# Scores of a pair of heads: block diagonal keys against two matmuls of 64 rows on two row groups

## The chip, the cores and the metric

The kernel runs on one core of one Trainium2 chip. The metric is the device time of one execution in microseconds (us). The kernel before was run three times: 2077.02, 2077.57 and 2078.26 us, median 2077.57 us. A profile of one execution shows which instruction ran on which engine and when. The engines are PE (TensorE, matmuls) with PEld (its weight loads, which overlap the matmuls), DVE (VectorE), ACT (ScalarE), POOL (GpSimd) and SP (SyncE, which issues transfers).

## The reference, cut to what matters

The network has four layers on 256 tokens of width 1024. Each layer is a feed-forward part, a token mixer and a second feed-forward part. Layers 0 and 3 use the mixer called DSA, layer 1 uses FoX, layer 2 uses MLA. All have 16 heads; DSA and FoX have 64 numbers per head, MLA has 96 in its queries and keys. What the change touches are scores of queries against keys:

```python
def causal_block_attention(q, k, v, scale, cum=None):            # FoX, MLA
    ...
        s = jnp.einsum('bqhd,bkhd->bhqk', q[:, lo:hi], k[:, :hi]).astype(jnp.float32) * scale
        ...
        p = jax.nn.softmax(jnp.where(mask, s, -jnp.inf), axis=-1).astype(v.dtype)
        outs.append(jnp.einsum('bhqk,bkhd->bqhd', p, v[:, :hi]))

def dsa_mixer(x, w_in, w_out, cos_p, sin_p):                      # DSA
    ...
        dots = jnp.einsum('bqhd,bkd->bqhk', qib, ki).astype(jnp.float32) * (IDX_DIM ** -0.5)
        idx_score = jnp.einsum('bqh,bqhk->bqk', wib, jax.nn.relu(dots))   # 8 index heads, one key
        ...
        _, sel = lax.top_k(idx_score, topk)
        ...
        logits = jnp.einsum('bqhd,bqkhd->bhqk', qb, ks).astype(jnp.float32) * scale
```

DSA has two kinds of scores: those of the indexer (8 index heads of 64, all against one shared key), whose weighted sum picks the 64 best keys of each query, and those of the 16 heads themselves.

## The kernel before, in words

Every product is a float32 product made of three passes: an operand is split into a high part and a low part (`split`, L189: ACT copies the high part, then DVE subtracts to get the low part), and the passes high·high, high·low, low·high are summed in PSUM (`mm3`, L157 to L161). Weights come from memory through SP's queue into `raw` tiles and are split too (`unit`, L127 to L147: ACT L144, DVE or POOL L145). Tokens are two tiles of 128 (t = 0, 1).

Heads are treated in eight pairs, two pairs to a group. `heads` (L439) runs the pairs one after the other. For pair p+1 it emits the score matmuls, then pieces of the projections of later groups and of the output product (the tables `PLAN_D`, `PLAN_F`, `OUTS` say how many), then for pair p the transposes of the softmax weights (`turn`), the softmax of pair p+1, more pieces, and the product with the values (`weigh`). What is emitted is then put in an order for each engine by a scheduler; every engine works through its own list in that order and waits where an operand is not ready.

One matmul of 128 rows holds both heads of a pair: rows 0 to 63 of the array are the first head's 64 numbers, rows 64 to 127 the second's. The queries of the pair are the stationary operand (128 rows, 128 queries). The keys are the moving operand and are block diagonal: `new_kz` (L494) gives a tile in which a head's rows are zero in the other head's columns (two POOL memsets, L497 and L498), and `put_kz` (L501) writes the keys of each head into its own block with a split of its own. So a pair takes, for each token tile, three matmuls with 2·128 columns (t = 0) or 2·256 columns (t = 1), into one bank of PSUM per token tile (`pair_scores`, L506). The scores of DSA's indexer use the same function, four pairs of index heads for each t; ACT then applies a ReLU to both heads at once (L560) and DVE adds them up with their weights (L564, L566). PSUM has two sets of four banks here, named psa and psb; scores, transposes and value products share psb.

Of the kernel before, what the change touches and what calls it, by code (L numbers as in the profile page):

```python
# [16 lines left out]
F32 = mybir.dt.float32  # L17
# [5 lines left out]
P = 128  # L23
D = 1024
SEQ = 256
# [6 lines left out]
HD = 64  # L32
# [19 lines left out]
class Net:  # L52
# [39 lines left out]
    def consts(self):  # L92
        """What the first products need; the rest comes in late_consts."""
# [7 lines left out]
        # the activation table and the tensor engine's clock are brought up while the loads run  # L101
# [67 lines left out]
    def flush(self):  # L169
        """Emits the transposes of x that wait for a place among other products."""  # L170
# [4 lines left out]
    def proj(self, us, t, out, flush=None):  # L175
        """out[tokens of tile t, n] = x @ w over the K tiles of us."""
# [6 lines left out]
    def projb(self, us, i, out, k0=0):  # L183
        """out[columns i*128.. of w, tokens] = (x @ w) transposed; us are the K tiles from k0."""
# [36 lines left out]
    def layer_norm(self, t, acc, mult, eps, last=False):  # L221
        """x <- LN(mult * x + acc); scaling the argument by two and eps by four changes nothing."""
# [677 lines left out]
```

## Time and profile before

| what | value |
|---|---|
| median of three runs | 2077.57 us |
| the profiled execution, first to last instruction | 2077.2 us |
| PE busy | 2021.1 us (97%), 13430 matmuls |
| PEld busy | 1853.2 us (89%) |
| DVE busy | 1271.0 us (61%) |
| ACT busy | 1030.3 us (50%) |
| POOL busy | 320.7 us (15%) |
| weights and other transfers | 362.98 MB, mean 175 GB/s |

The page gives the span of the profiled execution alone and no time around it; the runs' median is 0.4 us above that span. A busy time is the union of an engine's instructions; matmuls overlap each other, so the time that PE needs for one of them is read from start to start and not from its duration. The share of the whole span hides stages: the first DSA mixer's part from the indexer to its last pair is from about 226 to 345 us of the span, FoX's pairs start at about 772 us, the second DSA mixer's indexer at about 1757 us.

### The profile page before, as it was taken

Reading aid. Unit: us, or ns where it says so; the run is one execution under the profiler, and the core shown is the slowest. Engines: PE = TensorE matmul, PEld = TensorE weight load, DVE = VectorE, ACT = ScalarE, POOL = GpSimd, SP = SyncE. Lnnn points to the kernel's source line nnn. Section 1 sums busy time; section 2 is a strip of 40 time slices with the busy share of each in tenths; the row PEclk is TensorE's granted clock in tenths of the full one; section 3 lists DMA queues with packets and bytes.
Section 4 is the critical chain, followed back from the end, with each engine's and each line's share of the span. In section 5 each row is a group of like instructions: output and inputs, shape, how many; then the busy total and the mean of one; then the engine's idle time right before and its main releaser. Section 6 shows DMA issues by size and latency. Waiting matters only on the chain.

```text
span 2077.2 us, 34193 instructions
## 1 busy us (share of the span) xinstructions
PE 2021.1 (97%) x13430; PEld 1853.2 (89%) x13430; DVE 1271.0 (61%) x2069; ACT 1030.3 (50%) x1714; POOL 320.7 (15%) x454
## 2 busy tenths in 40 slices
PE   9999998999999998999999999899999999989998
PEld 8999986999899987799989998689989999978997
DVE  6455889544644469855465456964465546887453
ACT  5443476444444357644444436754444444675441
POOL 0002542000100145200110014400020005430000
PEclk9999999999999999999999999999999999999999
DMA  9754534665656454565665543566656564347550
GB/s 304 226 184 138 153 122 155 214 188 176 212 183 188 150 162 155 185 208 184 183 203 182 186 121 105 180 214 185 187 178 208 187 180 131 119 125 237 189 184 21
DMA packets 253025, 362.98 MB, mean 175 GB/s; under 512 B 11856, under 2 KB 204128, under 8 KB 252864
## 3 DMA queue, kind: packets, MB, share of 16 engines
q1 hardware_dynamic: 252080, 358.30, 54.7%
q0 software_dynamic: 784, 2.51, 0.4%
q8 instruction: 105, 1.72, 0.3%
q14 instruction: 56, 0.46, 0.1%
HBM read 359.69 MB, written 1.06 MB: 174 GB/s over the span
## 4 chain that ended last, share of the span: by engine, by line
PE 82%; DVE 12%; ACT 3%; issue 2%; POOL 0%; DMA 0%; SPq 0%; DVEq 0%; ACTq 0%; POOLq 0%
PE psa L166 14%; PE psa L167 14%; PE psa L165 14%; PE psb L159 8%; PE psb L160 8%; PE psb L161 8%; PE psa L159 5%; PE psa L161 5%; PE psa L160 5%; DVE slot L145 3%; DVE slot L191 2%; DVE s L406 2%; ACT s L403 1%; PE psb L202 1%; ACT slot L144 1%
## 5 line engine op out<-in xcount | busy, mean ns | idle before, releaser
L145 DVE TENSOR_TENSOR slot<-raw,slot 128x1024 fp32r<-128x1024 f32 (+4 forms) x724 | 773.1, 1089 | 617.5 <-ACT slot L144 614.9
L144 ACT CAST slot<-raw 128x1024 fp32r<-128x1024 f32 (+5 forms) x854 | 693.8, 849 | 652.0 <-issue 354.9
L166 PE MATMUL psa<-xh,slot 128*128 128x256 f32 x2496 | 707.6, 284 | 3.8 <-DVE slot L145 3.8
L165 PE MATMUL psa<-xh,slot 128*128 128x256 f32 x2496 | 707.4, 284 | 0.0
L167 PE MATMUL psa<-xl,slot 128*128 128x256 f32 x2496 | 707.1, 283 | 0.0
L166 PEld LDWEIGHTS psa<-xh,slot 128*128 128x128 f32 x2496 | 479.7, 192 | 7.6 <-DVE slot L145 4.6
L165 PEld LDWEIGHTS psa<-xh,slot 128*128 128x128 f32 x2496 | 479.6, 192 | 3.0
L167 PEld LDWEIGHTS psa<-xl,slot 128*128 128x128 f32 x2496 | 479.6, 192 | 0.0
L159 PE MATMUL psb<-slot,slot 128*128 128x512 f32 (+2 forms) x800 | 308.1, 385 | 9.0 <-DVE slot L191 4.8
L160 PE MATMUL psb<-slot,slot 128*128 128x512 f32 (+2 forms) x800 | 306.9, 384 | 1.9 <-DVE slot L191 1.9
L161 PE MATMUL psb<-slot,slot 128*128 128x512 f32 (+2 forms) x800 | 305.3, 382 | 1.2 <-DVE slot L191 1.2
L159 PE MATMUL psa<-slot,xh 128*128 128x256 f32 (+5 forms) x736 | 241.1, 328 | 0.0
L160 PE MATMUL psa<-slot,xh 128*128 128x256 f32 (+5 forms) x736 | 238.6, 324 | 0.0
L161 PE MATMUL psa<-slot,xl 128*128 128x256 f32 (+5 forms) x736 | 238.1, 324 | 0.0
L145 POOL TENSOR_TENSOR slot<-raw,slot 128x512 fp32r<-128x512 f32 (+4 forms) x130 | 183.5, 1428 | 306.1 <-ACT slot L144 297.1
L159 PEld LDWEIGHTS psb<-slot,slot 128*128 128x128 f32 (+1 forms) x800 | 150.9, 189 | 37.7 <-ACT slot L190 5.3
L78 POOL MEMSET slot<- 128x1 f32 (+1 forms) x88 | 8.5, 101 | 1118.4 <-PE psb L161 972.1
L161 PEld LDWEIGHTS psb<-slot,slot 128*128 128x128 f32 (+1 forms) x800 | 150.9, 189 | 30.9 <-DVE slot L191 1.5
L160 PEld LDWEIGHTS psb<-slot,slot 128*128 128x128 f32 (+1 forms) x800 | 151.2, 189 | 28.3 <-DVE slot L191 2.7
L159 PEld LDWEIGHTS psa<-slot,xh 128*128 128x128 f32 x736 | 140.6, 191 | 10.3 <-ACT xh L190 0.3
L160 PEld LDWEIGHTS psa<-slot,xh 128*128 128x128 f32 x736 | 140.6, 191 | 10.2
L161 PEld LDWEIGHTS psa<-slot,xl 128*128 128x128 f32 x736 | 140.4, 191 | 10.4
(150 smaller groups left out, 1696.7 us busy)
## 6 DMA issues: line engine op xcount, KB each, us to landing
raw<-in_ffn_w SPq DMA_DIRECT2D x528, 512.0 KB, 4.2
raw<-in_dsa_w_in SPq DMA_DIRECT2D x48, 512.0 KB, 3.8
raw<-in_w_out SPq DMA_DIRECT2D x32, 512.0 KB, 3.6
raw<-in_fox_w_in SPq DMA_DIRECT2D x24, 512.0 KB, 3.8
ln_g<-in_ln_g SPq DMA_DIRECT2D x12, 512.0 KB, 5.5
ln_b<-in_ln_b SPq DMA_DIRECT2D x12, 512.0 KB, 5.8
slot<-scratch_cum POOLq DMA_DIRECT2D x4, 512.0 KB, 5.4
raw<-in_mla_w_ukv SPq DMA_DIRECT2D x4, 512.0 KB, 3.9
```

The costliest lines, as they stand in the source:

```text
L144: nc.scalar.copy(h[:, c], raw[:, c])
L145: e.tensor_sub(l[:, c], raw[:, c], h[:, c].bitcast(F32))
L159: mm(out, sh, mh, start=start, stop=False)
L160: mm(out, sh, ml, start=False, stop=False)
L161: mm(out, sl, mh, start=False, stop=stop)
L165: mm(out, sh, mh, start=start, stop=False)
L166: mm(out, sl, mh, start=False, stop=False)
L167: mm(out, sh, ml, start=False, stop=stop)
L191: self.nc.vector.tensor_sub(lo, src, hi.bitcast(F32))
L202: self.nc.tensor.transpose(ps[:, i * P:(i + 1) * P], self.x[t][:, k * P:(k + 1) * P], self.ident)
L403: nc.scalar.activation(sv, sv, AF.Exp, bias=nb[:, c:c + 1], scale=scale, accum_out=l[:, c:c + 1])
L406: nc.vector.tensor_scalar(sv, sv, l[:, c:c + 1], None, op0=ALU.mult)
```

## The change

`pair_scores` no longer uses block diagonal keys. The keys of a pair lie as they come, 128 rows with both heads one above the other, and each pass is two matmuls of 64 rows: rows 0 to 63 (first head) and rows 64 to 127 (second head) of the array, each with its own weight load, and each writing its own bank of PSUM. The two token tiles of a head stand side by side in that bank (128 and 256 columns). In the indexer a call takes two banks where it took one, and the ReLU becomes two instructions, one for each bank. `new_kz` and `put_kz` go away: in DSA the queries and keys of a group are split together, in FoX the keys of a group are split at once. MLA's scores only change their form of call.

```diff
     def softmax(self, scores, bias, scale, cq=None):
-        pss = [scores(t) for t in range(NT)]
+        pss = scores(range(NT))
...
-                    nc.vector.tensor_tensor_reduce(out=sv, in0=pss[t][:, j, :], in1=bias(t, j), scale=1.0,
+                    nc.vector.tensor_tensor_reduce(out=sv, in0=pss[t][j], in1=bias(t, j), scale=1.0,
...
-    def new_kz(self, n=2):
-        """Block diagonal K of pairs: a head's rows are zero in the other head's columns."""
-        z = self.slot(2 * n, 2, SEQ, touch=False)
-        self.nc.gpsimd.memset(z[0:64, :, 1, :].bitcast(F32), 0.0)
-        self.nc.gpsimd.memset(z[64:128, :, 0, :].bitcast(F32), 0.0)
-        return z[:, :n], z[:, n:]
-
-    def put_kz(self, kz, c, src):
-        for j in range(2):
-            q = slice(64 * j, 64 * j + 64)
-            self.split(kz[0][q, :, j, c], kz[1][q, :, j, c], src[q])
-
     def pair_scores(self, qh, ql, kh, kl):
-        def scores(i):
-            ps = self.ps("b")
-            n = (i + 1) * P
-            o = ps[:, :2 * n].rearrange("p (j k) -> p j k", j=2)
-            q = slice(i * P, (i + 1) * P)
-            self.mm3(o, qh[:, q], ql[:, q], kh[:, :, :n], kl[:, :, :n], True, True)
-            return o
+        def scores(ts):
+            banks = [self.ps("b") for _ in range(2)]
+            out, o = [], 0
+            for t in ts:
+                n = (t + 1) * P
+                q = slice(t * P, n)
+                out.append([z[:, o:o + n] for z in banks])
+                o += n
+                for a, (st, mv) in enumerate(((qh, kh), (qh, kl), (ql, kh))):
+                    for j in range(2):
+                        r = slice(64 * j, 64 * j + 64)
+                        self.nc.tensor.matmul(out[-1][j], st[r, q], mv[r, :n], start=a == 0, stop=a == 2)
+            return out
         return scores
...
              self.split(qi[0][:, :, c], qi[1][:, :, c], p0.rearrange("p (k c) -> p k c", k=4))
-            self.put_kz(ki, c, p1[:, None, :P])
+            self.split(ki[0][:, c], ki[1][:, c], p1[:, :P])
...
         def index(t):
             n, sc = (t + 1) * P, scs[t]
             for i in range(4):
-                ps = self.pair_scores(qi[0][:, i], qi[1][:, i], *[z[:, 0] for z in ki])(t)
+                ps, = self.pair_scores(qi[0][:, i], qi[1][:, i], *ki)([t])
...
-                nc.scalar.activation(r[:, :, :n], ps, AF.Relu, scale=HD ** -0.5)
                 for j in range(2):
+                    nc.scalar.activation(r[:, j, :n], ps[j], AF.Relu, scale=HD ** -0.5)
...
 -                self.split(q[:, 0, :, c], q[:, 1, :, c], pt[:, 2:])
-                self.put_kz(kz, c, pt[:, :2])
+                self.split(qk[:, 0, :, c], qk[:, 1, :, c], pt.rearrange("p (k c) -> p k c", k=4))
...
 -                if isq:
-                    self.split(q[:, 0], q[:, 1], ps)
-                else:
-                    self.put_kz(kz, slice(None), ps)
+                self.split(qk[:, isq, 0], qk[:, isq, 1], ps)
```

The first place is PE's list in the first DSA mixer, where the scores of the third pair follow the value product of the first (L165 to L167). Names beginning with psb are PSUM banks. Before, the scores' last passes stand there, 256 columns for t = 0 and 512 for t = 1:

```order
L166 MATMUL psb_2960<-pth_2879,slot_2075 128x2x128
L167 MATMUL psb_2960<-ptl_2880,slot_2075 128x2x128
L160 MATMUL psb_2971<-slot_2486,slot_2489 128x256
L161 MATMUL psb_2971<-slot_2486,slot_2489 128x256
L159 MATMUL psb_2975<-slot_2486,slot_2489 128x512
L160 MATMUL psb_2975<-slot_2486,slot_2489 128x512
L161 MATMUL psb_2975<-slot_2486,slot_2489 128x512
L159 MATMUL psa_2993<-slot_2980,xh_1840 128x256
```

After the change the same place has twelve matmuls, which go to the banks of the two heads in turn:

```order
L167 MATMUL psb_2988<-ptl_2908,slot_2073 128x2x128
L508 MATMUL psb_2999<-slot_2512 128x128
L508 MATMUL psb_3000<-slot_2512 128x128
L508 MATMUL psb_2999<-slot_2512 128x128
L508 MATMUL psb_3000<-slot_2512 128x128
L508 MATMUL psb_2999<-slot_2512 128x128
L508 MATMUL psb_3000<-slot_2512 128x128
L508 MATMUL psb_2999<-slot_2512 128x256
L508 MATMUL psb_3000<-slot_2512 128x256
```

Six matmuls of 128 rows (the first of them stood a little earlier) have become twelve of 64 rows in one unbroken block. In the whole program there are 384 matmuls of 64 rows in 26 such blocks, two of them the indexers' (48 each), so that the lists change over to matmuls of 64 rows 26 times and back 26 times.

The second place is PE's list in the first indexer, where the second half of its calls begins. Before, matmuls of a projection (psa) stand between the calls:

```order
L161 MATMUL psb_2322<-slot_1968,slot_1966 128x256
L159 MATMUL psa_2382<-slot_2369,xh_1840 128x256
L159 MATMUL psb_2331<-slot_1968,slot_1966 128x512
L160 MATMUL psa_2382<-slot_2369,xh_1840 128x256
L161 MATMUL psa_2382<-slot_2369,xl_1841 128x256
L159 MATMUL psa_2382<-slot_2369,xh_1840 128x256
L160 MATMUL psb_2331<-slot_1968,slot_1966 128x512
L161 MATMUL psb_2331<-slot_1968,slot_1966 128x512
```

After the change nothing stands between them, and each call writes two banks:

```order
L508 MATMUL psb_2331<-slot_1968,slot_1966 128x128
L508 MATMUL psb_2332<-slot_1968,slot_1966 128x128
L508 MATMUL psb_2345<-slot_1968,slot_1966 128x256
L508 MATMUL psb_2346<-slot_1968,slot_1966 128x256
L508 MATMUL psb_2345<-slot_1968,slot_1966 128x256
L508 MATMUL psb_2346<-slot_1968,slot_1966 128x256
```

Seven projection matmuls that stood inside the first indexer now stand behind it.

The third place is ACT's list right behind the first indexer, where a group's queries and keys (psb_2409) are split. Before, the queries are split once and the keys twice, for the two halves of the rows:

```order
L190 CAST slot_2075<-psa_2382 128x256
L190 CAST slot_2075<-psb_2409 128x2x128
L144 CAST slot_2613<-raw_2612 128x512
L144 CAST slot_2696<-raw_2695 128x512 x2
L190 CAST slot_2072<-psb_2409 64x2x128
L190 CAST slot_2075<-psa_2420 128x256
L144 CAST slot_2703<-raw_2702 128x512
L190 CAST slot_2072<-psb_2409 64x2x128
```

After the change one instruction does it:

```order
L190 CAST slot_2073<-psa_2416 128x256
L190 CAST slot_2071<-psb_2443 128x4x128
L144 CAST slot_2713<-raw_2712 128x512 x2
L190 CAST slot_2073<-psa_2450 128x256
```

Three casts of a group's token tile are one, and the same holds for DVE's subtractions behind them.

## Rows read from the trace of the kernel before

**Rows 1.** The page: PE's busy time; columns are busy us, share, instructions.
```profile
PE 2021.1 (97%) x13430; PEld 1853.2 (89%) x13430; DVE 1271.0 (61%) x2069; ACT 1030.3 (50%) x1714; POOL 320.7 (15%) x454
```

**Rows 2.** Stretches, length; busy us (count) of PE, PEld, DVE, ACT, POOL; clock; DMA.
```profile
226.00:310.00 84.00, 78.80 (x601) 75.44 (x600) 74.52 (x218) 54.70 (x141) 38.10 (x52) 0.98 0.41 127
310.00:345.00 35.00, 29.72 (x154) 23.42 (x153) 31.96 (x77) 22.34 (x64) 7.79 (x7) 1.00 0.49 158
772.00:830.00 58.00, 50.31 (x367) 46.15 (x365) 53.06 (x140) 39.56 (x106) 34.24 (x35) 0.97 0.45 146
```

**Rows 3.** Chain of waits from 226 to 310 us, by line.
```profile
by line: DVE slot L145 18.8%; DVE slot L191 13.0%; DVE slot L566 8.6%; DVE slot L576 7.8%; issue 6.2%; DVE m L575 5.9%; PE psa L159 5.6%; PE psa L161 5.3%; PE psa L160 5.2%; DVE s L393 3.2%; ACT slot L144 2.5%; DVE ptl L191 2.4%; DVE nb L39
```

**Rows 4.** Waits of PE from 200 to 325 us: total, times, longest.
```profile
PE psb L159 <- DVE slot L191: 2.0, 1, 2.0
```

**Rows 5.** Timeline, score matmuls of the first indexer: start us, duration us, engine, line.
```profile
231.46 0.39 PE L161 MATMUL psb<-slot,slot 128*128 128x512 f32 x1
...
231.69 0.39 PE L159 MATMUL psb<-slot,slot 128*128 128x512 f32 x1
```

**Rows 6.** Timeline, weight loads that follow an idle PE, of two kinds.
```profile
229.94 0.19 PEld L159 LDWEIGHTS psb<-slot,slot 128*128 128x128 f32 x1 [1.32 <-ACT slot L190]
...
230.05 0.19 PEld L160 LDWEIGHTS psa<-slot,xh 128*128 128x128 f32 x1
...
290.46 0.14 PEld L416 LDWEIGHTS psb<-c_ident,s 128*128 128x128 f32 x1 [1.29 <-issue]
...
290.52 0.14 PEld L417 LDWEIGHTS psb<-c_ident,s 128*128 128x128 f32 x1
```

**Rows 7.** Timeline around two transposes of 16 rows in FoX (L673).
```profile
772.14 0.28 PE L167 MATMUL psa<-xl,slot 128*128 128x256 f32 x1
...
772.35 0.20 PEld L673 LDWEIGHTS psb<-c_ident,slot 16*128 16x128 f32 x2
772.35 0.29 PE L673 MATMUL psb<-c_ident,slot 16*128 16x16 f32 x2
772.57 0.19 PEld L159 LDWEIGHTS psb<-slot,slot 128*128 128x128 f32 x1
772.57 0.39 PE L159 MATMUL psb<-slot,slot 128*128 128x256 f32 x1
...
772.79 0.28 PE L160 MATMUL psb<-slot,slot 128*128 128x256 f32 x1
...
772.91 0.28 PE L161 MATMUL psb<-slot,slot 128*128 128x256 f32 x1
```

**Rows 8.** Weight loads by line and shape: count, busy us, mean ns.
```profile
L673 PEld LDWEIGHTS psb<-c_ident,slot 16*128 16x128 f32 x2 | 0.2, 136 | 0.1
...
L416 PEld LDWEIGHTS psb<-c_ident,s 128*128 128x128 f32 x16 | 2.2, 140 | 1.6 <-issue 1.5
```

**Rows 9.** DVE's subtractions of L191 by shape, 212 to 345 us, then 755 to 860.
```profile
L191 DVE TENSOR_TENSOR slot<-psb,slot 64x256 fp32r<-64x256 f32 x32 | 13.2, 418 | 1.8 <-ACT slot L190 1.3
...
L191 DVE TENSOR_TENSOR slot<-psb,slot 128x256 fp32r<-128x256 f32 x8 | 3.3, 417 | 0.2
...
L191 DVE TENSOR_TENSOR slot<-psb,slot 128x512 fp32r<-128x512 f32 x2 | 1.4, 684 | 0.0
...
L191 DVE TENSOR_TENSOR slot<-psa,slot 64x512 fp32r<-64x512 f32 x8 | 5.5, 687 | 2.5 <-ACT slot L190 2.4
...
L191 DVE TENSOR_TENSOR slot<-psa,slot 128x512 fp32r<-128x512 f32 x4 | 2.7, 685 | 3.2 <-ACT slot L190 3.1
```

**Rows 10.** Timeline of the first indexer: third and sixth ReLU, last score matmul.
```profile
230.85 0.38 ACT L560 ACTIVATE tok<-psb 128x256 f32<-128x256 f32 x1 [0.96 <-DVE slot L566]
...
233.53 0.39 PE L161 MATMUL psb<-slot,slot 128*128 128x512 f32 x1
...
233.78 0.60 ACT L560 ACTIVATE tok<-psb 128x512 f32<-128x512 f32 x1 [0.24 <-DVE slot L566]
```

**Rows 11.** POOL's memsets of key tiles in the whole span, first of two lines.
```profile
L497 POOL MEMSET slot<- 64x1024 f32 x12 | 11.4, 947 | 10.3 <-PE psa L161 9.1 <-ACT slot L144 0.8 <-PE psa L167 0.4
```

More of the change, by code (lines that the diff above doesn't have):

```diff
@@ L523, in dsa @@
         qi = qi[:, 0], qi[:, 1]
-        ki = self.new_kz(1)
+        ki = self.slot(2, SEQ)
+        ki = ki[:, 0], ki[:, 1]
         misc = self.slot(2048, dt=F32)
@@ L585, in project @@
             qw = self.cols(w_in, 256 * g, 256)
-            kz = self.new_kz()
-            qv = self.slot(2, 2, 2, SEQ)
-            q, v = qv[:, 0], qv[:, 1]
+            qk = self.slot(2, 4, SEQ)
+            v = self.slot(2, 2, SEQ)
             toks = []
@@ L598, in project @@
                 yield 1
-            ready[g] = (q, kz, v)
+            ready[g] = (qk, v)
             vals = self.values(w_in, 2 * D + 256 * g, v)
@@ L606, in project @@
                     nc.tensor.transpose(pt[:, i * P:(i + 1) * P], toks[t][:, i * P:(i + 1) * P], self.ident)
-                pt = pt.rearrange("p (k c) -> p k c", k=4)
-                self.split(q[:, 0, :, c], q[:, 1, :, c], pt[:, 2:])
-                self.put_kz(kz, c, pt[:, :2])
+                self.split(qk[:, 0, :, c], qk[:, 1, :, c], pt.rearrange("p (k c) -> p k c", k=4))
                 yield 1
@@ L613, in weights @@
             g, i = p // 2, p % 2
-            q, kz, v = ready[g]
-            rest = self.softmax(self.pair_scores(q[:, 0, i], q[:, 1, i], kz[0][:, i], kz[1][:, i]),
+            qk, v = ready[g]
+            rest = self.softmax(self.pair_scores(*(qk[:, z, y + i] for y in (2, 0) for z in range(2))),
                                  lambda t, j: sel[t], HD ** -0.5)
@@ L679, in project @@
             if g % 2 == 0:
-                both["ck"], both["q"] = self.slot(2, 4, SEQ, dt=F32), self.slot(2, 2, 2, SEQ)
-            ck, q = both["ck"][:, g % 2], both["q"][:, g % 2]
+                both["ck"] = self.slot(2, 4, SEQ, dt=F32)
+            ck, qk = both["ck"][:, g % 2], self.slot(2, 2, 2, SEQ)
             nc.gpsimd.dma_start(ck, self.a["s_cum"][4 * g:4 * g + 4].partition_broadcast(P))
-            kz = self.new_kz()
-            ready[g] = (q, kz, ck)
+            ready[g] = (qk, ck)
             for isq, o in ((0, D), (1, 0)):
@@ L691, in project @@
                         yield 1
-                if isq:
-                    self.split(q[:, 0], q[:, 1], ps)
-                else:
-                    self.put_kz(kz, slice(None), ps)
+                self.split(qk[:, isq, 0], qk[:, isq, 1], ps)
                 yield 1
@@ L699, in weights @@
             g, i = p // 2, p % 2
-            q, kz, ck = ready[g]
+            qk, ck = ready[g]
             b0 = b0s[p % 2]
@@ L708, in weights @@
             nc.vector.tensor_copy(cq, cumq[:, 2 * p:2 * p + 2, :].rearrange("p h t -> p t h"))
-            rest = self.softmax(self.pair_scores(q[:, 0, i], q[:, 1, i], kz[0][:, i], kz[1][:, i]),
+            rest = self.softmax(self.pair_scores(*(qk[:, y, z, i] for y in (1, 0) for z in range(2))),
                                  lambda t, j: b0[:, j, :] if t == 0 else cp[:, j, :], scale,
@@ L803, in weights, with scores @@
             q, k = qk[i]
-            def scores(t):
-                ps = self.ps("b").rearrange("p (j k) -> p j k", j=2)
-                c = slice(t * P, (t + 1) * P)
-                for j in range(2):
-                    self.mm3(ps[:, j], q[:, 0, j, c], q[:, 1, j, c], k[:, 0, j], k[:, 1, j], True, True)
-                return ps[:, :, :(t + 1) * P]
+            def scores(ts):
+                out = []
+                for t in ts:
+                    ps = self.ps("b").rearrange("p (j k) -> p j k", j=2)
+                    c = slice(t * P, (t + 1) * P)
+                    for j in range(2):
+                        self.mm3(ps[:, j], q[:, 0, j, c], q[:, 1, j, c], k[:, 0, j], k[:, 1, j], True, True)
+                    out.append([ps[:, j, :(t + 1) * P] for j in range(2)])
+                return out
             rest = self.softmax(scores, lambda t, j: self.diag if t == 0 else self.mask1, scale)
```

## The prediction, made before the changed kernel ran

> **What bounds the kernel now.** I read the busy times first, then busy time by stretch, then the chain of waits of the stretch where the change sits, then the timeline of single matmuls there. PE is busy 97% of the span [rows 1], so over the whole run time is PE time. In the stretches that the change touches this is less plain. From the first indexer to the fourth group's projections (226 to 310 us) PE is busy 78.80 of 84 us and DVE 74.52; from 310 to 345 us DVE is busy 31.96 of 35 and PE 29.72; in FoX's first 58 us DVE has 53.06 and PE 50.31 [rows 2]. The chain of waits from 226 to 310 us runs through DVE more than through PE: its two largest lines are the splits of weights (L145, 18.8%) and of activations (L191, 13.0%) [rows 3]. One of PE's longest waits, 2.0 us, is for such a split before the first scores [rows 4]. So two things can move the end: PE's time for the scores, and DVE's time for splits, the second only as far as PE idles (5.2 us in 226 to 310, 7.7 us in 772 to 830) [rows 2].
>
> **Part 1: the scores of the 24 pairs (8 in each of two DSA layers and FoX).** Start to start, a matmul of 512 columns takes 0.23 us [rows 5] and one of 256 columns 0.12 us [rows 7]. A pair before is three of each: 3 × 0.12 + 3 × 0.23 = 1.05 us. After, it is twelve matmuls of 64 rows, six with 128 and six with 256 columns, each with a weight load of its own. The columns streamed one after the other would be the same as before; only if two row groups work at once are they halved. The trace has no such pair, so I bound it by loads. After an idle time the next load starts 0.11 us after the first, 229.94 to 230.05 [rows 6]: a load of 128 queries in this number format keeps the loading path for 0.11 us. (Transposes need 0.06 us, 290.46 to 290.52.) Before, a load was hidden behind 256 or 512 columns; now it is as long as the whole matmul of 256 and longer than that of 128 columns.
>
> - Low end: loads and matmuls of the two halves run side by side, and each of the six passes takes 0.12 us, as a pass of 256 columns does now (its load alone needs 0.11): 0.72 us.
> - High end: the loads of the two halves queue behind one another, 12 × 0.11 = 1.32 us.
>
> To this comes the change-over between matmuls of 128 rows and of fewer rows. The trace has it once: two transposes of 16 rows between ordinary matmuls [rows 7]. The matmul before them starts at 772.14; without them the next would have started at 772.26. Its load starts only at 772.57, and since the matmul behind it starts at 772.79, it streams from 772.67. So the detour costs 0.41 us, of which two loads at the transposes' 0.06 are 0.12: 0.29 us for the way in and out. The loads there are not drawn ahead of the running matmul as everywhere else (772.35 instead of 772.14). The changed list has 24 such blocks for the pairs. The low end of this cost is 0, if a half array changes over without waiting.
>
> The Trainium skill, in "TensorEngine Tiling (Array Packing)", section "Key Properties", says that a change of tiling mode drains the array, while different tiles load and multiply in parallel. This trace agrees with the first half by the 0.29 us; no run here shows the second. By the page alone, whose drain has no price, a pair would cost 0.72 us plus a drain.
>
> Which end? The only row with two loads in sequence is at 0.11 us, but both of them fill the same rows of the array. Loads of separate rows have no row here, and I take them as side by side. A pair is then 0.72 + 0.29 = 1.01 us against 1.05, and 24 pairs give −1.0 us. The ends for 24 pairs: (0.72 − 1.05) × 24 = −7.9 us without a change-over, and (1.32 + 0.29 − 1.05) × 24 = +13.4 us with queued loads.
>
> **Part 2: the indexers (two).** On PE the same count holds for four calls at each t: 4 × 1.05 = 4.20 us become 4 × 0.72 + 0.29 = 3.17, so −1.0 us each if nothing waited. But a call now takes two of four psb banks where it took one, so a call can start only when the ReLUs of the call before last are done. These ReLUs wait for DVE: the third starts at 230.85 after 0.96 us of waiting for DVE, the sixth at 233.78 with 0.60 us of work [rows 10]. The eighth call, whose last matmul started at 233.53, now starts at 234.4 at the earliest and ends at about 235.0. That is 1.2 us late, and the seven projection matmuls that filled gaps and now come behind are 7 × 0.12 = 0.84 us: 2.0 us late in all. The second ReLU instruction of a call costs ACT little (half the columns each; 0.38 for 256, 0.60 for 512 columns). PE then runs into the 2.0 us wait for DVE before the first scores [rows 4], which swallows part of the delay. I take half, +1.0 us each, +2 us together; ends −2 and +4.
>
> **Part 3: splits.** In a DSA layer the keys' splits are 16 of the 32 DVE instructions of 64x256, 418 ns each (the other 16 belong to the value products and stay), and the queries' are 8 of 128x256 at 417. They become 8 of 128x512 at 684 [rows 9]: 16 × 0.418 + 8 × 0.417 − 8 × 0.684 = 4.55 us less DVE work. In FoX 8 of 64x512 at 687 become 4 of 128x512 at 685: 2.76 us less. Over two DSA layers and FoX DVE loses 11.9 us, and ACT a little less by the same counts. The two halves of a split also no longer follow each other from ACT to DVE and back. How much of this reaches the end is bounded by PE's idle time: 5.2 us per DSA layer before 310 us, 7.7 in FoX [rows 2]. Of the DVE time saved I take about half: −2.5 us per DSA layer and −1 in FoX, −6 us; ends 0 and −11.9.
>
> **Part 4: POOL.** The 24 memsets of 0.95 us [rows 11] vanish. POOL is busy 38.10 of 84 us there [rows 2], and its rotary work, queued behind them, is needed only by later transposes: 0, at best −1 us.
>
> **Sum.** −1.0 + 2 − 6 = −5 us against the profiled 2077.2, so 2072.2; the runs' median is 0.4 us above that span, so about 2073 us. Of the halving of streamed columns almost nothing is left in it: it goes into change-overs and load time, and what gain there is comes from DVE.
>
> **Rivals.**
>
> *A. Loads of the two halves queue (slower).* Place: the 24 blocks on PE. Price: +13.4 us there, and the indexers' calls get 0.28 us longer each (1.32 − 1.05 plus change-over), which mostly disappears in their waits, so +2.5 instead of +2. With more PE work, DVE's savings count less, −4. Sum +12, so 2089 us. It decides from a load spacing of about 0.09 us: then 12 loads and 0.29 exceed 1.05 by 0.32, and 24 × 0.32 = 7.7 outweighs the −4 of the other terms by more than measurement can tell. For it: the only pair of successive loads is 0.11 us apart [rows 6], and fewer rows do not make a load shorter, since 16 rows by 128 columns take 136 ns and 128 rows 140 [rows 8]. Against it: the two halves use separate rows of the array, which no two loads of this trace do.
> The Trainium skill, "TensorE: Matmul & The Clock Gate", section "LDWEIGHTS (loading the stationary operand)", says that loading time goes by columns and not by rows; the 136 and 140 ns agree. The change doubles the loads and leaves their columns, so by that rule, with loads in sequence, this rival's 13.4 us follow. Its section "Part 3: Packing small matmuls — row/col tiling" has matmuls of different row groups start some ns apart, which no run here shows.
>
> *B. Nothing but a wash.* PE is the bound even in these stretches (78.80 of 84), DVE's savings only lengthen DVE's idle time, pairs are even: −1 + 2 + 0 = +1, 2078.5 us. For it: PE's 97%. Against: DVE leads the chain.
>
> *C. The change does all that it can.* Side by side and no change-over: −7.9, indexers −1, splits −6: −15, about 2063 us. Against: the 0.29 us are in the trace, though for tiles of 16 rows.
>
> **Chances.** Forecast 0.40, own range 2068 to 2078; A 0.30; B 0.20; C 0.10. A measurement of this kernel can tell 0.2%, 4.2 us, from no change, so faster is below 2073.4. The forecast lies on that line: 0.25 of its 0.40 faster, 0.13 the same, 0.02 slower. A: 0.28 slower, 0.02 the same. B: 0.02 faster, 0.14 the same, 0.04 slower. C: faster. Together faster 0.37, same 0.29, slower 0.34. The range reaches into A and C: 2062 to 2090 us.
>
> **What would show it.** In a pair's block, loads of the two halves that start together and six passes in about 0.7 us (right), or loads 0.11 us apart and a block of 1.3 us or more (A). At each block's ends, a first load that starts only after the matmul before it, about 0.3 us in all; without that, C. In the indexers, waits of PE for the ReLU between 229 and 235 us; a granted clock below 1.00 there would add to part 2. In 226 to 310 us, DVE busy about 4.5 us less and PE idle less by half of that; if PE's idle stays while the scores take the same time, part 3 is wrong.

## The result and the profile after

The changed kernel takes 2091.56 us (median of four runs, 2090.34 to 2093.15) against 2077.30 us of the kernel before in the same session: a ratio of 1.0067, 95% interval 1.0053 to 1.0081. It is 14 us slower; 2073 us with a range up to 2090 were predicted. Neither the direction nor the range held. Rival A came near with 2089 us, but by loads that queue, and the trace below shows none; no rival has what was found. (In some sessions a single execution took hundreds of us longer; the medians here leave these out.)

The page of the changed kernel shows 15.9 us less busy time on DVE and 27.2 less on POOL, and 12.4 more on PE [rows 1]:

```profile
span 2088.8 us, 34519 instructions
...
PE 2033.5 (97%) x13622; PEld 1861.3 (89%) x13622; DVE 1255.1 (60%) x2029; ACT 1022.0 (49%) x1690; POOL 293.5 (14%) x438
```

PE's idle time, the span less its busy time, is 56.1 us before and 55.3 after. So the span grew with the time that PE is busy, and its waits did not grow in sum.

The extra time lies in three places only. Measured between the ends of the layer norms, the first DSA mixer went from 153.9 to 158.6 us, FoX from 133.3 to 138.1, the second DSA mixer from 151.1 to 154.5. MLA stayed within 0.1 us; the feed-forward parts moved by -2.6 to +1.6 us, -1.4 in all. Together that is the 11.6 us by which the two profiled spans differ (2077.2 and 2088.8). The medians are 2.7 us further apart: the profiled execution of the change took 2090.54 us, 1.0 below its median, and that of before must have taken about 2079 (an estimate), since the times of the other runs mostly lie 1.7 to 1.8 us above their spans.

The next view is the busy time by stretch; its first three rows answer to [rows 2]. The fourth and fifth cut the first DSA mixer of the changed kernel at its first pair's scores: the lead with the indexer, then the heads. The last is a part of the lead.

```profile
226.00:310.00 84.00, 78.92 (x649) 75.19 (x650) 67.32 (x203) 51.05 (x131) 31.20 (x45) 0.96 0.40 120
310.00:345.00 35.00, 30.01 (x157) 23.49 (x157) 27.74 (x69) 21.31 (x59) 8.16 (x7) 0.90 0.48 152
772.00:830.00 58.00, 53.54 (x418) 49.27 (x416) 49.56 (x136) 36.48 (x95) 24.73 (x29) 0.94 0.49 161
...
205.91:264.76 58.85, 56.64 (x454) 55.41 (x453) 42.77 (x105) 28.35 (x64) 26.69 (x48) 0.94 0.51 152
264.76:364.51 99.75, 88.91 (x588) 76.12 (x588) 80.90 (x209) 67.12 (x166) 31.63 (x36) 0.97 0.42 133
229.50:236.30 6.80, 6.80 (x36) 6.36 (x36) 6.56 (x20) 4.70 (x12) 1.50 (x2) 0.50 0.12 41
```

The same cut in the kernel before:

```profile
208.46:263.43 54.97, 53.34 (x427) 52.22 (x426) 44.52 (x111) 28.78 (x64) 28.76 (x49) 1.00 0.48 143
263.43:362.35 98.92, 88.25 (x541) 76.66 (x540) 86.56 (x221) 69.98 (x177) 33.95 (x39) 0.98 0.44 141
```

The lead is 3.9 us longer, at a granted clock of 0.94 where it was 1.00. The heads are 0.8 us longer although DVE works 5.7 us less in them. Over three mixers the leads gained 8.3 us (3.9 and 4.5 in DSA, nothing in FoX) and the heads 4.7 us, all of it in FoX (101.0 to 105.9). The granted clock is 0.50 (1.2 instead of 2.4 GHz, called half rate below) for 44.4 us of the three mixers, against 13.7 before, and for 59.1 us of the whole execution, against 26.8.

PE's waits, 200 to 364 us, answer to [rows 4]: total, times, longest.

```profile
PE psb L508 <- DVE slot L191: 3.0, 2, 2.1
PE psb L418 <- DVE slot L191: 2.7, 3, 1.7
PE psb L165 <- ACT pth L190: 2.3, 2, 1.8
```

L418 is a line of the turn: its last two transposes now wait for a bank that a split still reads. In the heads of the three mixers PE's idle time ahead of the turns' transposes grew from 4.3 to 11.6 us. Other waits shrank: in all, PE is idle for 29.8 us of these heads before and for 28.1 after.

One thing behaved as forecast. This is a pair's block on PE in the changed kernel, answering to [rows 7], then the loads in it as a summary (shortest, median and longest ns, first and last start):

```profile
273.68 0.28 PE L166 MATMUL psb<-pth,slot 128*128 128x256 f32 x1
273.80 0.28 PE L167 MATMUL psb<-ptl,slot 128*128 128x256 f32 x1
274.01 0.96 PE L508 MATMUL psb<-slot 64*128 64x128 f32 x12
274.90 0.39 PE L159 MATMUL psa<-slot,xh 128*128 128x256 f32 x1
275.12 0.28 PE L160 MATMUL psa<-slot,xh 128*128 128x256 f32 x1
```
```profile
L508 PEld LDWEIGHTS psb<-slot x12: 183/187/188, 274.0 to 274.6; 64*128 64x128 f32 x12
```

Twelve loads and twelve matmuls start within 0.7 us: the halves run side by side. In the trace the two matmuls of a pass start 3 to 4 ns apart. A pass follows 0.11 to 0.12 us after the one before, but 0.17 us after the first pass of either width. Then the edges: 273.80 to 274.01 is 0.21 us where 0.12 is normal, and so is the step out (274.69 to 274.90), and one more slow step of 0.22 follows, 274.90 to 275.12. Over the same stretch, last matmul ahead to second matmul behind, the kernel before needs 1.29 us:

```profile
305.12 0.28 PE L167 MATMUL psb<-ptl,slot 128*128 128x256 f32 x1
305.24 0.28 PE L159 MATMUL psb<-slot,slot 128*128 128x256 f32 x1
...
306.29 0.28 PE L159 MATMUL psa<-slot,xh 128*128 128x256 f32 x1
306.41 0.28 PE L160 MATMUL psa<-slot,xh 128*128 128x256 f32 x1
```

That is 1.29 against 1.32 us: the halved columns are used up by the change-over. The block on PE is not where 14 us are lost.

### The profile page after: what moved, and what is told of

It reads as the page before. It is cut to its first block, busy times and chain, and to the rows that moved or that the text cites. A ratio compares the mean times of both kernels' runs of the same rounds, so it can differ in the third digit from the quotient of the medians.

```text
span 2088.8 us, 34519 instructions
## 1 busy us (share of the span) xinstructions
PE 2033.5 (97%) x13622; PEld 1861.3 (89%) x13622; DVE 1255.1 (60%) x2029; ACT 1022.0 (49%) x1690; POOL 293.5 (14%) x438
## 4 chain that ended last, share of the span: by engine, by line
PE 85%; DVE 9%; ACT 3%; issue 2%; POOL 1%; DMA 1%; SPq 0%; DVEq 0%; ACTq 0%; POOLq 0%
PE psa L165 14%; PE psa L167 14%; PE psa L166 14%; PE psb L159 8%; PE psb L160 8%; PE psb L161 7%; PE psa L159 6%; PE psa L160 6%; PE psa L161 6%; DVE slot L145 3%; DVE s L406 1%; ACT s L403 1%; DVE slot L191 1%; PE psb L202 1%; PE psb L508 1%
## 5 line engine op out<-in xcount | busy, mean ns | idle before, releaser
L145 DVE TENSOR_TENSOR slot<-raw,slot 128x1024 fp32r<-128x1024 f32 (+4 forms) x724 | 768.8, 1083 | 618.1 <-ACT slot L144 615.3
L165 PE MATMUL psa<-xh,slot 128*128 128x256 f32 x2496 | 708.6, 284 | 0.0
L167 PE MATMUL psa<-xl,slot 128*128 128x256 f32 x2496 | 707.4, 283 | 0.0
L165 PEld LDWEIGHTS psa<-xh,slot 128*128 128x128 f32 x2496 | 480.2, 192 | 3.5 <-issue 0.2
L167 PEld LDWEIGHTS psa<-xl,slot 128*128 128x128 f32 x2496 | 480.1, 192 | 0.0
L159 PE MATMUL psb<-slot,slot 128*128 128x512 f32 (+1 forms) x736 | 284.4, 387 | 0.0
L160 PE MATMUL psb<-slot,slot 128*128 128x512 f32 (+1 forms) x736 | 283.8, 386 | 0.0
L161 PE MATMUL psb<-slot,slot 128*128 128x512 f32 (+1 forms) x736 | 283.0, 385 | 0.0
L145 POOL TENSOR_TENSOR slot<-raw,slot 128x512 fp32r<-128x512 f32 (+4 forms) x130 | 180.4, 1405 | 329.9 <-ACT slot L144 323.2
L161 PEld LDWEIGHTS psb<-slot,slot 128*128 128x128 f32 (+1 forms) x736 | 138.3, 188 | 28.2
L159 PEld LDWEIGHTS psb<-slot,slot 128*128 128x128 f32 (+1 forms) x736 | 138.5, 188 | 25.6
L160 PEld LDWEIGHTS psb<-slot,slot 128*128 128x128 f32 (+1 forms) x736 | 138.6, 188 | 24.7
L161 PEld LDWEIGHTS psa<-slot,xl 128*128 128x128 f32 x736 | 141.8, 193 | 10.4
```

Source lines behind the costliest of these rows:

```text
L145: e.tensor_sub(l[:, c], raw[:, c], h[:, c].bitcast(F32))
L159: mm(out, sh, mh, start=start, stop=False)
L160: mm(out, sh, ml, start=False, stop=False)
L161: mm(out, sl, mh, start=False, stop=stop)
L165: mm(out, sh, mh, start=start, stop=False)
L167: mm(out, sh, ml, start=False, stop=stop)
```

## The experiments

Differences below are against the kernel before in the same session (2077.3 to 2078.4 us). The last column is the time at half rate in the whole kernel (mean of its runs), worked out from the granted clock of each run, which is on record in steps of 0.001, or 4 us; the kernel before has 25 us.

| kernel | median us | difference, us | ratio, 95% interval | half rate, us |
|---|---|---|---|---|
| the change | 2091.56 | +14.3 | 1.0067 (1.0053 to 1.0081) | 57 |
| change, indexer of before | 2089.86 | +12.2 | 1.0052 (1.0032 to 1.0072) | 53 |
| the same in more rounds | 2088.99 | +10.6 | 1.0050 (1.0038 to 1.0063) | 56 |
| before, indexer of the change | 2079.95 | +2.3 | 1.0012 (1.0002 to 1.0021) | 43 |
| change, other DSA plan | 2086.96 | +9.3 | 1.0042 (1.0027 to 1.0057) | 43 |
| change, matmuls of 128 rows | 2091.78 | +14.1 | 1.0063 (1.0045 to 1.0082) | 40 |
| change, splits by halves | 2095.04 | +16.8 | 1.0077 (1.0062 to 1.0092) | 57 |
| change's splits, blocks of before | 2071.40 | -6.8 | 0.9962 (0.9949 to 0.9976) | 23 |
| twelve 128-row matmuls, bank to a token tile | 2088.47 | +10.4 | 1.0044 (1.0027 to 1.0061) | 37 |
| change, other DSA plan, indexer of before | 2079.26 | +1.0 | 1.0008 (0.9995 to 1.0022) | 35 |
| the same, FoX's plan too | 2079.66 | +1.4 | 1.0009 (0.9998 to 1.0019) | 37 |
| four banks, indexer of before | 2084.88 | +6.8 | 1.0035 (1.0023 to 1.0047) | 35 |
| four banks, both plans | 2087.12 | +9.0 | 1.0041 (1.0028 to 1.0053) | 34 |
| 64-row blocks in DSA's heads alone, other plan | 2076.82 | -1.5 | 0.9990 (0.9982 to 0.9999) | 36 |
| before, other DSA plan | 2074.49 | -3.8 | 0.9985 (0.9976 to 0.9994) | 28 |
| the same, indexer of the change | 2076.93 | -1.5 | 0.9992 (0.9983 to 1.0001) | 37 |

The diffs below are cut to the lines that matter, against the changed kernel.

### Indexer or heads

```diff
-                ps, = self.pair_scores(qi[0][:, i], qi[1][:, i], *ki)([t])
+                ps = self.diag_scores(qi[0][:, i], qi[1][:, i], *[z[:, 0] for z in ki])(t)
```

> The indexer alone goes back to block diagonal keys, one bank and one ReLU per call; the heads keep matmuls of 64 rows. In the changed kernel the three changed mixers took 158.60, 138.14 and 154.52 us (DSA, FoX, DSA), before 153.89, 133.30, 151.07. Theory 'banks' (the indexer's two banks per call stop PE for 2.3 and 3.3 us and the clock falls there): each DSA mixer falls by 3 to 4 us, FoX stays near 138, total about 2085 us. Rival 'lists' (the scheduler's new order in the heads brings the waits): DSA falls by at most 1 us each, total 2089 or more. Rival 'half array' (matmuls of 64 rows keep the clock low): the low clock leaves the indexer but stays in the heads; DSA falls by 1 to 2 us each, total about 2088.

The reverse, the changed indexer alone in the kernel before:

> The kernel before with the new indexer alone (48 matmuls of 64 rows in a row, two banks and two ReLUs per call); the heads keep block diagonal keys. 'Banks': each DSA mixer is 3 us slower than before, FoX as before (133.3), total about 2083 us. 'Lists': DSA within 1 us of before, total 2077 to 2079. 'Half array': the clock is low for about 7 us in each indexer and in the heads as before, total about 2080.

The first gave 2089.86, the second 2079.95. So the heads alone lose about 11 us (12.2, and 10.6 when run again) and the indexer alone 2.3. Yet it does lengthen the lead: 59.0 and 58.7 us with it in the second run, 55.1 and 56.5 without it in the first, near the 55.0 and 55.6 of the kernel before. The lines of the first indexer in the changed kernel show how:

```profile
224.29 0.55 PE L508 MATMUL psb<-slot,slot 64*128 64x128 f32 x6
226.90 5.49 PE L508 MATMUL psb<-slot,slot 64*128 64x128 f32 x42 [2.06 <-DVE slot L191]
```

After the first call PE waits 2.06 us for banks that a split still reads, and soon after, from 229.5, the clock is 0.50 for 6.8 us. With the heads of before, much of what the lead loses comes back behind it: DSA's heads take 1.6 and 2.6 us less there (in the kernel before, scores of the first two pairs wait 2.0 us for a split [rows 4]). A single profile must not be pressed, though: FoX, with the same instructions in the same order as in the kernel before, took 130.3 us in this run and 133.3 there.

### The order, by a plan

```diff
-PLAN_D = [(0, 1), (1, 1), (0, 1), (0, 1), (1, 1), (0, 1), (0, 0), (0, 0)]
+PLAN_D = [(0, 1), (1, 1), (1, 0), (1, 0), (1, 1), (1, 0), (0, 0), (0, 0)]
```

> The changed kernel with DSA's table of fillers altered: for the third, fourth and sixth pair the piece of projection stands ahead of the transposes of the softmax weights and not behind them. 'Lists': the waits of PE at transposes that directly follow a score block (1.25 and 1.67 us, 1.90 us) go, each DSA mixer falls by 2 to 4 us, FoX stays at 138, total about 2085 us. 'Banks' and 'half array': no change in the heads, total 2090 to 2092.

> The changed kernel with both mends that each gave something alone: the indexer of before (block diagonal keys, one bank, one ReLU; alone -1.7) and DSA's plan with four groups' work put ahead of a pair's turn rather than behind it (alone -4.6). 'Lists': the two stand in different stages and add, 2083 to 2087. If the run to run scatter of some 3 us a kernel is all that they showed, 2088 to 2093.

> The kernel with both mends (indexer of before, DSA's plan), and FoX's plan changed in the same sense: work of later groups ahead of a pair's turn ((3,1),(2,0) x4) rather than split around it ((2,2),(1,1) x4). 'Lists': FoX loses some of its +4.85 us over before: 2078 to 2084 in all. If FoX's loss is in the clock after 64-row matmuls alone, the plan changes nothing there: 2083 to 2088.

2086.96 and, with the old indexer, 2079.26; FoX's plan adds nothing (2079.66). So DSA's plan is worth 5.0 us with the changed indexer and 9.5 to 11.1 with the old one. I read this first as a repair of the order that the new blocks had been given. The control below takes 3.8 us of it back.

### The row groups against 128 rows

```diff
-                        self.nc.tensor.matmul(out[-1][j], st[r, q], mv[r, :n], start=a == 0, stop=a == 2)
+                        self.nc.tensor.matmul(out[-1][j], st[:, q], mv[:, :n], start=a == 0, stop=a == 2)
```

> The changed kernel with each matmul of 64 rows replaced by one of all 128 rows at the same place, so that each score is the sum of both heads' and not one head's; the lists of all engines are the same instruction for instruction. A block of twelve should take 12 loads of 0.11 us, about 1.3 us, instead of 0.68, and no change-over: 24 blocks and two indexers add about 0.35 x 24 + 2 x 2 = 12 us of PE time. 'Half array': the clock stays up as before (low for at most 14 us in the three mixers, 44 us in the changed kernel), which gives back 9 us: total about 2094. 'Lists' and 'banks': the longer blocks fill part of the waits, the low clock stays with the waits that remain: total 2096 to 2102.

2091.78, the same as with 64 rows, with all engines' lists unchanged. Its block:

```profile
277.94 0.28 PE L167 MATMUL psb<-ptl,slot 128*128 128x256 f32 x1
278.05 1.54 PE L507 MATMUL psb<-slot 128*128 128x128 f32 x12
279.43 0.28 PE L159 MATMUL psa<-slot,xh 128*128 128x256 f32 x1
279.55 0.28 PE L160 MATMUL psa<-slot,xh 128*128 128x256 f32 x1
```

1.61 us against 1.32: side by side saves 0.29 us a pair, 7 us for 24. That none of it shows in the total is in part chance: the run with 128 rows spends less time at half rate, 34.1 us of the three mixers instead of 44.4, and 40 of the whole instead of 57. At the price found further down (0.41 us for each) that is worth 4 to 7 us. So a part for half-filled arrays in the clock can't be excluded, but the loss is there without them.

### Splits or blocks

```diff
-                self.split(qk[:, 0, :, c], qk[:, 1, :, c], pt.rearrange("p (k c) -> p k c", k=4))
+                self.split(q[:, 0, :, c], q[:, 1, :, c], pt[:, 2:])
+                self.put_kz(kz, c, pt[:, :2])
```

> The changed kernel with its heads' score blocks left as they are (64-row matmuls, a bank to each head), but the keys split per head in halves of 64 rows as before (three splits where the change has one per token tile in DSA, and per column half in FoX), without memsets; the indexer stays the changed one. 'Splits': if the loss comes from the splits (the lists were laid out anew because they became fewer and shorter), this gives it back: 2076 to 2082. 'Blocks': if it comes from the score blocks (both token tiles of a head in one bank, softmax steps and turns earlier in the lists than their data), it stays: 2088 to 2096, the three mixers 10 to 16 us over before. 'Half array' (64-row matmuls themselves hold the clock down): stays slow too, 2088 to 2096.

```diff
-            banks = [self.ps("b") for _ in range(2)]
...
+                o = self.ps("b")[:, :2 * n].rearrange("p (j k) -> p j k", j=2)
+                both = [z[:, None, :n].to_broadcast([P, 2, n]) for z in (kh, kl)]
+                self.mm3(o, qh[:, q], ql[:, q], *both, True, True)
```

> The changed kernel with its single splits, but every score block in the shape of before: matmuls over all 128 rows whose moving side reads the pair's keys once for each head, both heads side by side in one bank, a bank to each token tile; the indexer likewise. Both heads then get the sum of the two heads' scores. 'Splits': the loss stays, 2086 to 2094. 'Blocks': it goes, and the shorter DVE list shows its worth: 2070 to 2080. 'Half array': it goes too, 2070 to 2080; it is told from 'blocks' by the run with 128-row matmuls in the changed banks, which stayed at 2091.8.

2095.04 and 2071.40: the blocks, clearly. The second run prices the two parts apart. The splits, with the memsets gone, are worth -6.8 us; the new blocks, with the indexer's, cost 20 to 21 us on top. In its heads (283.5 us over three mixers, against 300.1 after the change and 295.4 before) PE's idle time ahead of turns is 6.0 us, and the clock is at half rate for 10.2 us. (Its profiled execution, 2067.03 us, is one of its fastest.)

How the new blocks bring waits shows in DVE's timeline at one place. First the changed kernel, at the fourth softmax of the first DSA mixer, whose scores' last pass started at 284.89:

```profile
285.67 0.68 DVE L191 TENSOR_TENSOR slot<-psb,slot 128x512 fp32r<-128x512 f32 x1
286.27 1.48 DVE L145 TENSOR_TENSOR slot<-raw,slot 128x512 fp32r<-128x512 f32 x1
287.67 0.41 DVE L191 TENSOR_TENSOR slot<-psb,slot 64x256 fp32r<-64x256 f32 x1
288.01 0.27 DVE L393 CUSTOM_DVE_ANT_0 s<-psb,slot 128x128 f32<-128x128 f32 x1
...
288.51 0.43 DVE L191 TENSOR_TENSOR slot<-psb,slot 64x256 fp32r<-64x256 f32 x1 [0.23 <-ACT slot L190]
288.97 0.29 DVE L393 CUSTOM_DVE_ANT_0 s<-psb,slot 128x128 f32<-128x128 f32 x1
```

The same place with the blocks of before, whose last pass started at 282.58:

```profile
283.16 1.00 DVE L191 TENSOR_TENSOR slot<-psb,slot 128x512 fp32r<-128x512 f32 x2
284.09 0.27 DVE L393 CUSTOM_DVE_ANT_0 s<-psb,slot 128x128 f32<-128x128 f32 x1
...
284.96 0.43 DVE L191 TENSOR_TENSOR slot<-psb,slot 64x256 fp32r<-64x256 f32 x1
```

In the changed list a weight split (L145, 1.48 us) stands ahead of the value product's two splits and of the reductions (L393). So the softmax starts 3.12 us after the last pass instead of 1.51 (2.18 in the kernel before), and the bank of the value product is free only at 288.9. The turn waits for that bank; these are its lines on PE, first in the changed kernel, then with the blocks of before:

```profile
286.41 0.33 PE L416 MATMUL psb<-c_ident,s 128*128 128x128 f32 x1 [1.25 <-DVE slot L191]
...
289.09 0.41 PE L418 MATMUL psb<-c_ident,s 128*128 128x128 f32 x2 [1.67 <-DVE slot L191]
```
```profile
283.90 0.33 PE L416 MATMUL psb<-c_ident,s 128*128 128x128 f32 x1 [0.93 <-DVE slot L191]
...
284.75 0.39 PE L418 MATMUL psb<-c_ident,s 128*128 128x128 f32 x2
```

The delay is the rule, not a single case. From the start of a pair's last score matmul to its first reduction the median over eight pairs is, in the three mixers, 0.34, 0.16 and 0.27 us before (for some pairs token tile 0 is reduced while token tile 1 is multiplied); -0.04, 0.73 and -0.10 with the changed splits and old blocks; 1.25, 1.93 and 1.03 after the change.

### Banks or short matmuls

```diff
+                o = self.ps("b")
+                out.append([o[:, j * n:(j + 1) * n] for j in range(2)])
+                for j in range(2):
+                    self.mm3(out[-1][j], qh[:, q], ql[:, q], kh[:, :n], kl[:, :n], True, True)
```

> The changed kernel with the twelve matmuls of a block made of all 128 rows (each head then gets the sum of both heads' scores), as in the earlier run at 2091.8, but a bank to each token tile with both heads in it, as before, in place of a bank to each head; the indexer likewise. 'Banks' (the reductions of token tile 0 must wait until the block stops writing their bank, which with a bank to each head is the block's end): the loss goes, 2071 to 2078, and the first reduction stands at the start of the block's last matmul as before (median about 0 us rather than 0.8 to 1.25 after it). 'Short matmuls' (twelve of 128 and 256 columns in place of six of 256 and 512, which the order is laid out for): it stays, 2086 to 2093.

```diff
-                out.append([z[:, o:o + n] for z in banks])
+                out.append([self.ps("b")[:, :n] for _ in range(2)])
```

> The 64-row score blocks of the change, with a bank to each head and token tile (four in place of two), and the indexer of before. 'Banks' by waiting: token tile 0's reductions can start in the middle of the block, 2076 to 2084 (against 2089.9 with two banks and the same indexer), if the four banks held at once do not cost as much elsewhere: then 2086 to 2096 with waits of the turn and of projections' transposes on banks. 'Short matmuls': no gain, 2086 to 2092.

> The same with the plans of DSA and FoX changed so that later groups' work stands ahead of a pair's turn (with two banks this stood at 2079.7). 'Banks': 2070 to 2078, better than before. If the four banks cost more than the wait they take away: 2080 to 2088.

2088.47: mostly short matmuls. With a bank to each token tile the first reduction comes 0.37, 0.95 and 0.40 us after the last matmul's start (0.80, 1.00 and 0.51 with a bank to each head, same 128-row matmuls), but the list still has the weight split ahead of it:

```profile
288.66 0.68 DVE L191 TENSOR_TENSOR slot<-psb,slot 128x512 fp32r<-128x512 f32 x1
289.26 1.45 DVE L145 TENSOR_TENSOR slot<-raw,slot 128x512 fp32r<-128x512 f32 x1
290.64 0.41 DVE L191 TENSOR_TENSOR slot<-psb,slot 64x256 fp32r<-64x256 f32 x1
290.97 0.27 DVE L393 CUSTOM_DVE_ANT_0 s<-psb,slot 128x128 f32<-128x128 f32 x1
```

So twelve matmuls in place of six are enough for the scheduler to put DVE's work in another order. Of the 17 us by which this kernel stands above the one with six matmuls, 24 x 0.33 = 8 us are PE's own (1.61 against 1.28 us a block); the rest comes with the order, the first indexer's longer lead (58.9 against 54.4 us) and the lower clock (37 against 23 us at half rate) among it. That share can't be carried over one to one to the 64-row kernel, whose block is 0.3 us shorter.

With four banks the first reduction comes 0.68 us ahead of the last matmul's start in all three mixers, earlier than ever, and the turns' waits fall to 1.7 us. But the next scores then wait for banks, 14.6 us in the three mixers' heads against 4.05 after the change. PE's waits with four banks, 200 to 362 us (L527 are the score matmuls):

```profile
PE psb L527 <- DVE m L393: 3.9, 4, 2.4
PE psb L202 <- DVE x L247: 1.8, 2, 1.0
```

2084.88: of the 10.6 to 12.2 us that the heads cost, 3.8 to 5.4 come back. The plans on top make it no better.

### A control, and FoX apart

> The kernel before with that plan for DSA and nothing else. If the plan repairs the order that the changed blocks were given, it has nothing to repair here: 2077 to 2081. If it is better for any kernel, so that its gain of 4.6 in the changed kernel says nothing on the blocks: 2072 to 2075.

> The 64-row score blocks in DSA's heads alone, with DSA's plan that puts later groups' work ahead of a pair's turn; the indexer and FoX's heads are those of before. If the change's loss in FoX (+3 to +5 us in every profile with its blocks there) belongs to the blocks, and DSA's plan gives back what they cost there (its two layers stood 1.6 to 1.7 us under before with the old indexer): 2072 to 2076, better than before. If the plan's gain was scatter: 2077 to 2082.

> The changed kernel with the indexer of before once more, in more rounds (2089.9 in four runs that lay 7 us apart). With DSA's other plan the old indexer gave 7.7 us, about what it takes out of the lead of DSA's two mixers (some 3.8 each). If it gives the same under the plan of the kernels compared: 2083 to 2086, and the heads alone then cost 5 to 8 us. If the heads lose what the indexer gives: 2088 to 2092 again.

> The kernel before with the changed indexer alone and DSA's other plan (2074.5 with the old indexer). If the longer lead reaches the end whatever follows: 2080 to 2083. If the heads of before swallow it, as under the old plan (2079.95 against 2078.4): 2075 to 2077.5.

The plan makes the kernel before faster too, by 3.8 us. That is most of the 5.0 us that it gives the changed kernel, but not of the 9.5 to 11.1 us with the old indexer: there 6 to 7 us belong to the order that the new blocks had been given. The plan gives a second base for the parts. Under it DSA's new heads, blocks and splits together, cost 2.3 us (2076.82 against 2074.49), FoX's 2.5 more (-1.5 to +1.0), and the indexer alone 2.3 (-3.8 to -1.5), but 8.3 on top of both heads (+1.0 to +9.3). Under the plan of the change the heads alone cost 10.6 to 12.2, the indexer alone 2.3, both 14.3. So the parts add under one plan and not under the other. That a delay costs more once others have used up the slack would explain it, but no run shows it. The control, 2074.49 us, beats both kernels compared, and it has nothing of the change.

## Why the prediction was wrong, point by point

**Part 1, scores on PE: right, and too small a question.** "1.01 us against 1.05" is 1.08 by the same count (1.32 less two normal steps of 0.12), so 24 such pairs would cost +0.7 us where -1.0 stood. The first two pairs of a mixer share one block and save about 0.3 us, so the sum is near zero. Of the 1.08 us the six passes take 0.80 (0.72 was taken) and the change-over 0.28 (0.29). Loads side by side were the right choice: rival A falls. The change-over is what the transposes of 16 rows had shown [rows 7], so C falls too. Here the Trainium skill, "TensorEngine Tiling (Array Packing)", section "Key Properties", agrees in both halves: the change of mode costs 0.09, 0.09 and 0.10 us of extra steps, and loads of different tiles overlap.

**Part 2, indexers: +2, measured +2.3 alone, under either plan.** That is luck. The wait of 2.06 us for a bank is there, but for a split; the waits for ReLUs, 0.17 to 0.33 us of the weight loads, are small. Each lead is 3.9 to 4.5 us longer, the lower clock included; the prediction had 2.0 late, half of it swallowed. A larger delay and a larger share swallowed cancelled. The wait of [rows 4] was also misread: it stands not before the first scores, which start at 263.43 us, but inside the second pair's:

```profile
267.03 0.62 PE L159 MATMUL psb<-slot,slot 128*128 128x512 f32 x1 [2.03 <-DVE slot L191]
```

**Part 3, splits: -6, measured -6.8 with the old blocks and without the memsets.** In the changed kernel DVE does less, as counted [rows 9]:

```profile
L191 DVE TENSOR_TENSOR slot<-psb,slot 128x512 fp32r<-128x512 f32 x10 | 6.8, 684 | 1.8 <-ACT slot L190 1.8
L191 DVE TENSOR_TENSOR slot<-psb,slot 64x256 fp32r<-64x256 f32 x16 | 6.7, 419 | 5.4 <-ACT slot L190 5.3
```

But undoing the splits there costs only 2.5 us (2095.04 against 2091.56, each less its before). That a shorter DVE list helps less when the softmax starts late is an argument, not shown.

**Part 4** was not tested apart: the memsets are gone in every run without the old splits, so the -6.8 us contain what they were worth.

**The step that failed is the sum.** It priced a block by PE's time in it and then added the parts. It had no term for what the twelve matmuls do to the order of everything else, and none for the clock that PE is granted then; "a granted clock below 1.00" stood only among the signs. The section on the change showed PE's lists; DVE's list around the reductions was not looked at, where the weight split had moved ahead of them. The cost of both, with the indexer's, is the step from 2071.4 to 2091.6. The sign check in "What would show it" gave a warning: from 226 to 310 us DVE is busy 7.2 us less (74.52 to 67.32) and PE's idle time stays (5.2 to 5.1) [rows 2]. I had taken that as a sign against part 3; since the splits are worth 6.8 us with the old blocks, it points to a chain through DVE that starts later.

**Waits and clock.** Two profiles of one kernel (the change with the indexer of before) tell them apart. They have the same instructions in the same order on every engine, and differ in the clock. FoX's heads, first run and second:

```profile
774.13:878.17 104.04, 92.09 (x600) 78.38 (x599) 89.70 (x225) 65.01 (x161) 36.42 (x39) 0.97 0.46 151
776.36:885.94 109.58, 97.58 (x600) 82.85 (x599) 88.79 (x225) 64.95 (x161) 36.42 (x39) 0.91 0.44 143
```

PE is idle for 12.0 us in both, and at half rate for 6.8 and 20.5 us. So 13.7 us at half rate cost 5.5 us, 0.41 us each. With this price the heads of the three mixers can be taken apart (an estimate):

| heads of the three mixers | us | PE idle | half rate |
|---|---|---|---|
| changed splits, old blocks | 283.5 | 20.7 | 10.2 |
| before | 295.4 | 29.8 | 13.7 |
| the change | 300.1 | 28.1 | 30.7 |

From old blocks to new ones, 16.6 us, 7.4 are idle time and about 8.4 the clock. Against the kernel before the idle time fell by 1.8 us, and about 7 us of clock more than make up for that. For the whole kernel the table of runs gives 57 us at half rate against 25, about 13 us of the 14.3; over all the runs, each against the mean of its kernel, the price comes out at 0.34, which makes it 11. So the new blocks took back in waits what the splits had saved, and most of the loss against the kernel before goes with the lower clock.

What stays open is what lowers the clock. In the changed kernel each of the seven half-rate stretches in the three mixers comes soon after a wait of PE of 1.8 to 3.0 us, or within one. But the run with matmuls of 128 rows, with the same lists, has some 17 us less at half rate, so the 64-row matmuls, or the shorter time that PE has work, may have a part. A row-group block with the old order was not tried.

## What to carry to other kernels

Where a scheduler lays out the lists, a new form of a matmul is also a new order: compare the list of the engine that reads the result, and find what now stands ahead of the first reader. Ask when the first half of a result can be read: in these traces a bank that takes two token tiles is read only after the second. A gain on PE of 0.3 us a pair says little while the softmax behind the new blocks starts 1.1 to 1.3 us later than behind the old ones (medians). And when a span grows while PE's idle time does not, compare the granted clock before looking for waits.

## What the runs showed of the hardware

The two halves of a pass start 3 to 4 ns apart, their loads too, and loads of successive passes start 0.11 to 0.12 us apart. Passes of 128 and of 256 columns both follow each other at that distance, except that 0.17 us lie behind the first pass of either width; no pass of 128 columns comes faster than the loads. The Trainium skill, "TensorE: Matmul & The Clock Gate", section "Part 3: Packing small matmuls — row/col tiling", has row groups start some ns apart; this trace agrees. Leaving a 64-row block costs two slow steps, 0.21 and 0.22 us instead of 0.12: the load of the next 128-row matmul starts only with it (274.89, with the matmul at 274.90), and it is not drawn ahead.

In the changed kernel no pair's first reduction in DSA or FoX starts before the pair's last score matmul has started (0.20 us after it at the earliest), although token tile 0 is complete after half of the matmuls. The Trainium skill, "PSUM — Partial Sum Buffer", section "PSUM bank collisions raise a hardware error", forbids two engines in one bank at once, and a list that keeps to it has to wait. With a bank to each head and token tile the first reduction comes 0.68 us ahead of the last matmul's start (median), as that rule would have it.

The same instructions in the same order took 2082.7 and 2090.4 us from the first to the last in two executions, with 49.4 and 66.5 us at half rate.
